# The first modulation as split products for half of its weights, with x transposed to SBUF ahead of it

## The chip, the cores and the metric

The kernel runs on one core of a Trainium2 chip. The metric is device time in microseconds (us) of that core, from the start of the program to its end. The time before is the median of three runs, 1361.34 us (1361.11 to 1365.02).

The engines are named as in the profile: PE (TensorE, matrix products and transposes), PEld (its weight loads), DVE (VectorE), ACT (ScalarE), POOL (GpSimd), and SP, whose queue issues most DMAs. An engine works through its own queue in order. SBUF is the on-chip memory, PSUM the accumulator memory that TensorE writes.

## The reference

The kernel computes a trunk of two layers on 512 tokens of width 1024, in fp32. Layer 0 mixes tokens by differential attention (four heads; 256 context tokens are keys and values too) on one half of the width and by a Fourier transform on the other, layer 1 by a long convolution; each layer ends in a gated feed-forward part with a convolution. The change touches the very beginning:

```python
def ada_params(cvec, w, b):
    m = jax.nn.silu(cvec) @ w + b
    return jnp.split(m[..., None, :], N_MOD, axis=-1)      # N_MOD = 6 pieces of 1024

def modulate(x, shift, scale):
    return layer_norm(x) * (1 + scale) + shift
...
sh1, sc1, g1, sh2, sc2, g2 = ada_params(c, mod_w[0], mod_b[0])
h_lat = modulate(x, sh1, sc1)                               # 512 x 1024
csh1, csc1, ... = ada_params(c_ctx, mod_w[0], mod_b[0])
h_ctx = modulate(ctx, csh1, csc1)                           # 256 x 1024
p = h_lat @ w_in                                            # query, key, value, Fourier part
kv_c = h_ctx @ w_in[:, DA_W:3 * DA_W]                       # key and value of the context
```

Piece 0 of the modulation is the shift, piece 1 the scale, piece 2 the gate `g1`; pieces 0 and 1 are wanted for two vectors, `c` and `c_ctx`. The filter of the convolution in layer 1 begins with three small products, each followed by a sine (`hdn = jnp.sin(fr * (... @ w + b))`); these too are computed in the first 45 us of the kernel.

## The kernel before

*Split products.* Large products are not computed on fp32 operands. An operand x is taken apart into a high part, x rounded to the type fp32r, and a low part, x minus the high part, also as fp32r. `split` (L212) does so: ScalarE copies with a cast (L213), VectorE subtracts (L210, in `sub`). `mm3` (L239) then forms three products, low x high, high x low and high x high, into one PSUM bank. `wsplit` (L231) does it for a raw weight tile of 128x2048 in two halves of 128x1024. Raw weight tiles come from `raw` (L195), which has three buffers and loads on SP's queue.

*Order.* The code is written as Python generators that are stepped in turn, but the order in which an engine's instructions stand is set by a scheduler, which takes the program in the order written as priority. `behind` (L216) tells it that what is issued inside shall stand behind the instructions listed in `self.fence`. A tile pool gives each tag a number of buffers; a new tile in a full tag waits for the readers of the oldest.

*Start* (`start`, L410). SP's queue loads the eight raw chunks of pieces 1 and 0 (two k rows of 128x1024 each, `load_mods`) and x as two tiles of 128x2x1024 (`load_x`), interleaved. `cT` holds silu of both vectors as two columns for each of eight k. `mods(piece)` (L454) forms, for each chunk, four fp32 products 2x512 (`pm`, L461: `cT[:, k]` against a half row), 32 over both pieces; copies the two-row result to `m2`, transposes it back to columns in `pmt` (L471), and adds the bias. `norm` normalizes x row-wise in place by `plain_norm` (L523: two statistics, square root on ScalarE, reciprocal, and one VectorE `tensor_scalar`, L531). `filter_head` (from L583) runs the filter's three products (`pz`, L595), each followed by `sine`: eight VectorE operations on `sa` (L574 to L579) and the sine itself on ScalarE (L580). `lift(k)` transposes the k-th column block of x into PSUM (`pt`, L491; three banks), `fill(k)` applies scale and shift out of PSUM, on ScalarE for even k (L501) and on VectorE for odd, and splits the result into `th` and `tl`. Three `lift` come ahead of the last chunks of piece 0, the other five one by one between the `fill`s.

*Attention's first stage* (`attention`, L693). `project_qk(0)` forms head 0's query (`pq`) by `mm3` over eight k, with rotary embedding in `roped` (L775 to L779, on VectorE). Then the context rows `xc` are loaded and normalized, and `gate_rows` (L533) forms the gate as sixteen fp32 products of one row, copies it to SBUF, and spreads it over the partitions (`pmr`, L545 and L546). The key follows (`pk`), then `context` (L555): in two halves, eight transposes of `xc` into a PSUM bank and four conversions, each a ScalarE activation to `fc` (two buffers), a cast to `ch` and a VectorE low part to `cl`. The context's key product (`pkc`) reads `ch` and `cl` k by k. Then come the values (`project_tokens`), and the attention proper, the rest of the layer and layer 1, none of which the change rewrites. In the background VectorE sums further modulation pieces into `acc` (`mod_jobs`, L278 and L280).

## Time and profile before

| | |
|---|---|
| time, median of three runs | 1361.34 us (1361.11 to 1365.02) |
| profiled execution, its own time | 1366.71 us |
| its span | 1364.9 us |
| TensorE busy | 1318.6 us, 97% |
| VectorE busy | 971.3 us, 71% |
| ScalarE busy | 585.9 us, 43% |
| GpSimd busy | 32.9 us, 2% |
| mean granted TensorE clock | 0.984 |

The trace is of one execution, which was 5.4 us longer than the median, so differences between stages are taken within it. A busy TensorE isn't one at its peak: the granted clock, in shares of 2.4 GHz, stands in a column of its own, and at 0.5 the same product takes twice as long. An fp32 product stands in the trace as two records, a product of fp32r as one. An idle time in brackets is that of the same engine just before the instruction, with what ended it.

### The profile page before, as it was taken

The page shows a single profiled execution, that of the slowest core. Times are in us where ns is not written, and L with a number is a line of the kernel's source. Part 1 is how long each engine was busy: PE and PEld are TensorE (multiplying, and loading weights), DVE is VectorE, ACT ScalarE, POOL GpSimd, SP SyncE. Part 2 cuts the span into 40 slices and gives each one's busy share as a digit, 9 for nine tenths or more (in the row PEclk, how much of TensorE's full clock was granted, in tenths as well). Part 3 has the DMA queues.
Part 4 walks back from the last instruction along what each step waited for, and adds up shares of the span by engine and source line. Part 5 has one row for each costly group of instructions (what it writes and reads, how often), then busy time and mean ns, then how long its engine had stood idle before and what let it go on. Part 6 is the DMA issues. An engine that isn't in the chain of part 4 may idle for free. (4 is left out here: it accounts for less than half of the span.)

```text
span 1364.9 us, 16745 instructions
## 1 busy us (share of the span) xinstructions
PE 1318.6 (97%) x6719; PEld 1092.7 (80%) x6719; DVE 971.3 (71%) x1418; ACT 585.9 (43%) x878; POOL 32.9 (2%) x44
## 2 busy tenths in 40 slices
PE   7999999989999999999999999999999999999997
PEld 1478889878887888888888878888888888888886
DVE  4667788676879975896666688899777555577545
ACT  2544545555545533433345533334563333333332
POOL 0000000000011000000000100000000000000000
PEclk9899999989999999999999999999999999999999
DMA  9562024053744554663243653232555222233201
GB/s 354 183 232 99 32 104 151 1 203 126 258 167 153 204 199 172 218 217 111 99 157 108 249 175 116 93 109 88 197 195 185 93 93 93 96 104 109 93 31 62
DMA packets 42253, 195.52 MB, mean 143 GB/s; under 512 B 4204, under 2 KB 5822, under 8 KB 29375
## 3 DMA queue, kind: packets, MB, share of 16 engines
q1 hardware_dynamic: 39522, 184.57, 38.6%
q0 software_dynamic: 1824, 8.66, 1.9%
q10 hardware_dynamic: 829, 1.21, 0.3%
q8 instruction: 53, 0.87, 0.2%
q14 instruction: 25, 0.20, 0.0%
HBM read 181.85 MB, written 12.58 MB: 142 GB/s over the span
## 5 line engine op out<-in xcount | busy, mean ns | idle before, releaser
L1086 ACT ACTIVATE u<-pf,pp 128x512 f32<-128x512 f32 x90 | 70.2, 781 | 123.5 <-PE pf L244 70.2
L1087 DVE SCALAR_TENSOR_TENSOR u<-pf,pp,u 128x511 f32<-128x511 f32 x90 | 67.0, 745 | 30.2 <-ACT u L1086 30.0
L278 DVE SCALAR_TENSOR_TENSOR acc<-mw,cT,acc 128x1024 f32<-128x1024 f32 x66 | 84.6, 1282 | 5.0 <-DMA mw<-in_modw 4.7
L966 DVE TENSOR_TENSOR wo<-wo,g 128x1024 f32<-128x1024 f32 x60 | 72.0, 1217 | 5.8 <-DMA wo<-in_dao 3.7
L210 DVE TENSOR_TENSOR sl<-hid,sh 128x512 fp32r<-128x512 f32 x39 | 26.8, 690 | 62.2 <-ACT sh L213 62.2
L213 ACT CAST sh<-hid 128x512 fp32r<-128x512 f32 x39 | 24.0, 621 | 103.8 <-PE py L997 100.7
L1088 DVE SCALAR_TENSOR_TENSOR u<-pf,pp,u 128x511 f32<-128x511 f32 x90 | 67.2, 746 | 1.9
L1038 DVE SCALAR_TENSOR_TENSOR y<-x,py 128x1024 f32<-128x1024 f32 x16 | 19.5, 1219 | 26.3 <-PE py L997 26.3
L863 ACT ACTIVATE e<-blk,nm 128x768 f32<-128x768 f32 x32 | 28.6, 900 | 22.2 <-DVE nm L860 18.0
L1040 ACT ACTIVATE junk<-y,sv 128x1024 f32<-128x1024 f32 x16 | 18.4, 1152 | 41.3 <-DVE sv L1039 41.3
L461 PE MATMUL pm<-mw,cT 128*2 128x512 f32 x64 | 31.1, 637 | 3.9 <-DVE cT L448 3.9
L860 DVE TENSOR_REDUCE nm<-blk 128x1 f32<-128x768 f32 x32 | 29.2, 946 | 4.5 <-PE blk L855 4.3
L1114 DVE TENSOR_TENSOR hid<-u 128x512 f32<-128x512 f32 x44 | 30.7, 697 | 2.1 <-ACT u L1111 0.2
L1070 DVE TENSOR_SCALAR f<-pt,mod,mod 128x128 f32<-128x128 f32 x48 | 16.4, 403 | 20.3 <-ACT f L1072 20.3
L1111 ACT ACTIVATE u<-u 128x512 f32<-128x512 f32 x44 | 27.4, 623 | 0.0
L461 PEld LDWEIGHTS pm<-mw,cT 128*2 128x2 f32 x64 | 5.2, 88 | 25.4 <-issue 21.4
L854 PE MATMUL blk<-ks,ql 128*128 128x512 f32 (+1 forms) x64 | 21.5, 353 | 1.2 <-DVE ks L210 0.7
L1072 ACT ACTIVATE f<-pt,mod,mod 128x128 f32<-128x128 f32 x48 | 18.0, 455 | 9.2 <-PE pt L1058 9.2
L1052 ACT ACTIVATE y<-x,sv 128x1024 f32<-128x1024 f32 x12 | 13.9, 1155 | 18.2 <-DVE sv L1051 18.1
L855 PE MATMUL blk<-ks,qh 128*128 128x512 f32 (+1 forms) x64 | 21.1, 348 | 0.0
L1042 DVE SCALAR_TENSOR_TENSOR x<-y,sv,ln 128x1024 f32<-128x1024 f32 x16 | 20.6, 1285 | 0.7
L1043 DVE SCALAR_TENSOR_TENSOR x<-x,sv,ln 128x1024 f32<-128x1024 f32 x16 | 20.5, 1284 | 0.6
(1102 smaller groups left out, 4402.3 us busy)
## 6 DMA issues: line engine op xcount, KB each, us to landing
mw<-in_modw SPq DMA_DIRECT2D x48, 1024.0 KB, 5.0
wi<-in_ffi SPq DMA_DIRECT2D x44, 1024.0 KB, 5.0
wo<-in_ffo SPq DMA_DIRECT2D x22, 1024.0 KB, 5.0
wv<-in_hyxv SPq DMA_DIRECT2D x8, 1024.0 KB, 5.0
xd<-x SPq DMA_DIRECT2D x12, 512.0 KB, 2.8
x<-xd SPq DMA_DIRECT2D x12, 512.0 KB, 4.6
wqk<-in_daqk SPq DMA_DIRECT2D x4, 1024.0 KB, 5.9
wo<-in_dao SPq DMA_DIRECT2D x4, 1024.0 KB, 5.0
```

What stands on the lines that cost most here:

```text
L210: return e.tensor_tensor(lo, src, hi.bitcast(F32), op=ALU.subtract)
L213: return self.nc.scalar.copy(hi, src), self.sub(lo, src, hi, eng)
L278: nc.vector.scalar_tensor_tensor(acc, ws, c, acc, op0=ALU.mult, op1=ALU.add)
L461: nc.tensor.matmul(ps[0:2, h], self.cT[:, k], w, start=(k == 0), stop=(k == KD - 1))
L860: nc.vector.tensor_reduce(nm[s], ps[s], axis=AX.X, op=ALU.max, negate=True)
L863: nc.scalar.activation(e[s], ps[s], AF.Exp, bias=nm[s], accum_out=su[s])
L966: nc.vector.tensor_tensor(w[:, ws], w[:, ws], gate, op=ALU.mult)
L1086: nc.scalar.activation(out, ps, AF.Identity, scale=w[:, 1:2], bias=w[:, 3:4])
L1087: nc.vector.scalar_tensor_tensor(out[:, 1:], ps[:, : L - 1], w[:, 0:1], out[:, 1:], op0=ALU.mult, op1=ALU.add)
L1088: return nc.vector.scalar_tensor_tensor(out[:, : L - 1], ps[:, 1:], w[:, 2:3], out[:, : L - 1], op0=ALU.mult, op1=ALU.add)
L1111: nc.scalar.activation(u[:, 0], u[:, 0], AF.Gelu)
L1114: nc.vector.tensor_tensor(hid[j // 2][:, j % 2], u[:, 0], u[:, 1], op=ALU.mult)
```

## The change

It has six parts.

1. Chunks 0 and 2 of each of the pieces 1 and 0 (`PARTED`) are taken apart by `wsplit`, and each of their fp32 products becomes two fp32r products: the high part of the weights against four columns (`c4`: high and low part of both vectors), and the low part against two. The sum has four rows for 512 columns, so `m2` and `pmt` are wider, and the two parts are added with the bias.
2. The norm of x ends with a ScalarE activation in place of the VectorE operation (`plain_norm` with `act`).
3. All eight column blocks of x are transposed and copied to SBUF (`f1`) before the modulation's last chunks; `fill` works from there. For k = 2 and 5 the low part is formed on GpSimd.
4. The three steps of the filter's head are spread among the chunks, each behind the last product of the chunk ahead of it. The second half of the query weights is split behind `fill(1)`.
5. The context rows are loaded by one DMA at the end of the start, into the buffer that `cl` takes over later (`Late`), and normalized behind the last `fill`, by ScalarE too. `context` issues all sixteen transposes first, then the eight conversions.
6. `gp`, a column wanted by the attention's last step, is formed behind a fence, and not ahead of the start's first products; the PSUM pool of the start waits tile by tile (`reuse_waits`), and one more raw chunk of piece 0 goes to a buffer of `raw`.

```diff
--- before.py
+++ after.py
+    PARTED = {1: (0, 2), 0: (0, 2)}
...
-            cl = hp.pool.tile([128, KD, LC], F32R, name="cl")
+            xc = hp.pool.tile([128, 2, D], F32, tag="cl", name="xc")
+            cl = Late(lambda: hp.pool.tile([128, KD, LC], F32R, tag="cl", name="cl"))
...
-            if n < 3:
+            if n < 3 or n == 7:
...
-            for i in range(2):
-                mw[piece, k + i] = w[:, i]
+            mw[piece, k] = w
...
+        up = {0: self.bank("sc", 3, "pt")}
+        c4 = self.cst.tile([128, KD, 4], F32R, name="c4")
+        self.split(c4[:, :, 0:2], c4[:, :, 2:4], self.cT)
...
-                self.plain_norm(xn[i][:, t], f"{i}{t}")
+                self.plain_norm(xn[i][:, t], f"{i}{t}", True)
...
             ps = self.bank("pm", 2, f"pm{piece}", 2)
-            m2 = self.cst.tile([128, 2, 512], F32, tag=("gate", "acc")[piece], name=f"m2{piece}")[0:2]
+            m2 = [self.cst.tile([128, D], F32, tag=t, name=f"m2{piece}{t}")[0:4, 0:512] for t in ("gate", "acc")]
+            mm = nc.tensor.matmul
             for c in range(0, KD, 2):
+                parted = c // 2 in self.PARTED[piece]
+                if parted:
+                    hs, ls = self.wsplit(mw[piece, c].rearrange("p a d -> p (a d)"), f"mw{piece}{c}")
-                    for k in (c, c + 1):
-                        w = mw[piece, k][:, h * 512 : (h + 1) * 512]
-                        nc.tensor.matmul(ps[0:2, h], self.cT[:, k], w, start=(k == 0), stop=(k == KD - 1))
+                    half = slice(h * 512, (h + 1) * 512)
+                    for i in range(2):
+                        k = c + i
+                        f, e = k == 0, k == KD - 1
+                        if parted:
+                            mm(ps[0:4, h], c4[:, k], hs[i][:, half], start=f, stop=False, skip_group_check=True)
+                            j = mm(ps[0:2, h], c4[:, k, 0:2], ls[i][:, half], start=False, stop=e, skip_group_check=True)
+                        else:
+                            w = mw[piece, c][:, i, half]
+                            j = mm(ps[0:2, h], self.cT[:, k], w, start=f, stop=e, skip_group_check=True)
+                self.fence = (j,)
                 yield
-            nc.scalar.copy(m2[:, 0], ps[0:2, 0])
-            nc.vector.tensor_copy(m2[:, 1], ps[0:2, 1])
+            nc.scalar.copy(m2[0], ps[0:4, 0])
+            nc.vector.tensor_copy(m2[1], ps[0:4, 1])
             pt = self.bank("po", 1, f"pmt{piece}")
             o = MODB0 + piece * 8
...
-                        pt[:, 2 * x : 2 * x + 2], m2[:, h, m * 128 : (m + 1) * 128], self.ident[0:2, 0:2]
+                        pt[:, 4 * x : 4 * x + 4], m2[h][:, m * 128 : (m + 1) * 128], self.ident[0:4, 0:4]
                     )
             for i in range(2):
-                nc.vector.tensor_tensor(ms[i], pt[:, i:16:2], self.pp[:, o : o + 8], op=ALU.add)
-                if piece == 1:
-                    nc.vector.tensor_scalar(ms[i], ms[i], 1.0, None, op0=ALU.add)
+                nc.vector.tensor_tensor(ms[i], pt[:, i:32:4], self.pp[:, o : o + 8], op=ALU.add)
+                nc.vector.scalar_tensor_tensor(
+                    ms[i], ms[i], 1.0 if piece == 1 else 0.0, pt[:, i + 2 : 32 : 4], op0=ALU.add, op1=ALU.add
+                )
...
-        up = {}
-
         def lift(k):
-            up[k] = self.bank("sc", 3, "pt")
...
+            up[k] = p.tile([128, L], F32, tag=f"f1{k}", name=f"f1{k}")
+            nc.scalar.copy(up[k], ps)
-            f = p.tile([128, L], F32, tag="f1", bufs=2, name=f"f1{k}")
+            f = up[k]
             if k % 2:
-                nc.vector.tensor_scalar(f, up[k], sc, sh, op0=ALU.mult, op1=ALU.add)
+                nc.vector.tensor_scalar(f, f, sc, sh, op0=ALU.mult, op1=ALU.add)
             else:
-                nc.scalar.activation(f, up[k], AF.Identity, scale=sc, bias=sh)
-            self.split(th[:, k, :], tl[:, k, :], f)
-
-        ms, mb = mods(1), mods(0)
+                nc.scalar.activation(f, f, AF.Identity, scale=sc, bias=sh)
+            self.fence = self.split(th[:, k, :], tl[:, k, :], f, "pool" if k in (2, 5) else "dve")
+
+        ms, mb, hd = mods(1), mods(0), self.filter_head(p)
+        step(hd, 1)
         step(ms, 1)
-        for _ in self.filter_head(p):
-            pass
+        step(hd, 1)
         step(ms, 1)
+        step(hd, 1)
         norm(1)
-        step(ms, 3)
+        step(ms, 1)
+        step(hd, 1)
+        step(ms, 1)
+        step(ms, 1)
+        step(hd, 1)
+        step(mb, 1)
+        step(mb, 1)
         norm(2)
-        step(mb, 2)
-        for k in range(3):
+        step(mb, 1)
+        for k in range(KD):
             lift(k)
-        step(mb, 3)
-        self.first = self.wsplit(self.raw(I["daqk"][0], "wqk0"), "wqk0")
+        step(mb, 1)
+        step(mb, 1)
+        raw = self.raw(self.I["daqk"][0], "wqk0")
+        self.first = [], []
+
+        def weights(i):
+            h, l = (self.wtile(f"w{x}", [128, 1024], f"wqk0{x}{i}") for x in "hl")
+            self.split(h, l, raw[:, i * 1024 : (i + 1) * 1024])
+            for a, t in zip(self.first, (h, l)):
+                a.append(t)
+
+        weights(0)
+        nc.sync.dma_start(xc, I["ctx"].rearrange("(t p) d -> p t d", p=128))
         for k in range(KD):
             fill(k)
-            if k + 3 < KD:
-                lift(k + 3)
+            if k == 1:
+                with self.behind():
+                    weights(1)
+        with self.behind():
+            for t in range(2):
+                self.plain_norm(xc[:, t], f"0{t}", True)
         return th, tl
-    def plain_norm(self, x, name):
+    def plain_norm(self, x, name, act=False):
...
-        nc.vector.tensor_scalar(x, x, mu, r, op0=ALU.subtract, op1=ALU.mult)
+        if act:
+            nc.vector.scalar_tensor_tensor(mu, mu, -1.0, r, op0=ALU.mult, op1=ALU.mult)
+            nc.scalar.activation(x, x, AF.Identity, scale=r, bias=mu)
+        else:
+            nc.vector.tensor_scalar(x, x, mu, r, op0=ALU.subtract, op1=ALU.mult)
...
+        pts = []
         for half in range(2):
-            pt = self.bank("blk", 2, "blk", 3).rearrange("p a b -> p (a b)")
+            pts.append(self.bank("blk", 2, "blk", 3).rearrange("p a b -> p (a b)"))
...
-                    self.nc.tensor.transpose(pt[:, o : o + 128], xc[t][:, c : c + 128], self.ident)
-            for k in range(4):
-                kk = 4 * half + k
-                sc, sh = (self.mods[0, x, 1][:, kk : kk + 1] for x in (1, 0))
-                f = self.p.tile([128, LC], F32, tag="e0", bufs=2, name="fc")
-                self.nc.scalar.activation(f, pt[:, k * LC : (k + 1) * LC], AF.Identity, scale=sc, bias=sh)
-                self.split(ch[:, kk, :], cl[:, kk, :], f)
+                    self.nc.tensor.transpose(pts[half][:, o : o + 128], xc[:, t, c : c + 128], self.ident)
+        cl.make()
+        for kk in range(KD):
+            k = kk % 4
+            sc, sh = (self.mods[0, x, 1][:, kk : kk + 1] for x in (1, 0))
+            f = self.p.tile([128, LC], F32, tag="e0", bufs=2, name="fc")
+            self.nc.scalar.activation(f, pts[kk // 4][:, k * LC : (k + 1) * LC], AF.Identity, scale=sc, bias=sh)
+            self.split(ch[:, kk, :], cl[:, kk, :], f)
...
-            nc.tensor.matmul(ps, fw[0:66, 0] if i == 0 else fw[:, i], cur, start=True, stop=True)
+            with self.behind():
+                nc.tensor.matmul(ps, fw[0:66, 0] if i == 0 else fw[:, i], cur, start=True, stop=True)
...
+            yield
...
-        gp = self.sm.tile([128, 1], F32, name="gp")
-        nc.vector.tensor_scalar(gp, self.pp[:, SG0 : SG0 + 1], POST, None, op0=ALU.mult)
...
-        xc = []
...
-                for t in range(2):
-                    xc.append(p.tile([128, D], F32, tag=f"pt{t}", name=f"xc{t}"))
-                    nc.sync.dma_start(xc[t], I["ctx"][t * 128 : (t + 1) * 128])
-                    self.plain_norm(xc[t], f"0{t}")
...
+        self.gp = self.sm.tile([128, 1], F32, name="gp")
+        with self.behind():
+            nc.vector.tensor_scalar(self.gp, self.pp[:, SG0 : SG0 + 1], POST, None, op0=ALU.mult)
...
+class Late:
+    def __init__(self, make):
+        self.tile = None
+        self.new = make
+
+    def make(self):
+        self.tile = self.new()
+
+    def __getitem__(self, at):
+        return self.tile[at]
```

The first place is on TensorE, in the modulation: how the split products stand among the fp32 ones. `pm` is the sum of one piece, `mw..h` and `mw..l` are high and low part of a chunk's half, `pz` is the filter head's product, `pt` a transposed block of x. Before:

```order
L461 MATMUL pm_134<-mw_102,cT 2x512 x4
L461 MATMUL pm_247<-mw_106,cT 2x512 x4
L461 MATMUL pm_247<-mw_108,cT 2x512 x2
L595 MATMUL pz<-hd_160,fw 128x256
L461 MATMUL pm_247<-mw_108,cT 2x512
L471 MATMUL pmt_218<-ident,m_135 128x2 x8
L461 MATMUL pm_247<-mw_108,cT 2x512
```

After:

```order
L472 MATMUL pm_264<-mw00h_271,c_131 4x512
L473 MATMUL pm_264<-mw00l_268,c_131 2x512
L472 MATMUL pm_264<-mw00h_271,c_131 4x512
L473 MATMUL pm_264<-mw00l_272,c_131 2x512 x2
L476 MATMUL pm_264<-mw_108,cT 2x512 x2
L641 MATMUL pz<-hd_181,fw 128x256
L476 MATMUL pm_264<-mw_108,cT 2x512
L487 MATMUL pmt_241<-ident,m21gate 128x4 x4
L487 MATMUL pmt_241<-ident,m21acc 128x4 x4
L476 MATMUL pm_264<-mw_108,cT 2x512
L506 MATMUL pt<-ident,xin_104 128x128 x3
L472 MATMUL pm_264<-mw04h_303,c_131 4x512 x2
```

In place of fp32 products of whole chunks, the last five fp32r products of chunk 0 of piece 0 stand in a row, and behind them two fp32 products ahead of the third `pz`. The transposes of the first piece's sums (`pmt`) and the first ones of x follow in between.

The second place is on VectorE, at the same time: the third sine of the filter's head (`sa`, lines 616 to 624 in the code after) and what stands around it. `mw00l` is a low part of the weights, `mod` the modulation's columns. Before, the second sine with the statistics and the norm of x:

```order
L527 BN_STATS st_240<-xin_104 128x6
L578 SCALAR_TENSOR_TENSOR sa_161<-sa_161 128x256
L464 COPY m_135<-pm_134 2x512
L578 SCALAR_TENSOR_TENSOR sa_161<-sa_161 128x256
L263 RECIPROCAL st_233<-st_233 128x1
L529 BN_AGGR st_240<-st_240 128x2
L578 SCALAR_TENSOR_TENSOR sa_161<-sa_161 128x256
L531 TENSOR_SCALAR xin_104<-xin_104,st_233 128x1024
L579 TENSOR_SCALAR sa_161<-sa_161 128x256
L263 RECIPROCAL st_240<-st_240 128x1
L531 TENSOR_SCALAR xin_104<-xin_104,st_240 128x1024
```

After, the second and the third:

```order
L623 SCALAR_TENSOR_TENSOR sa_182<-sa_182 128x256
L211 TENSOR_TENSOR mw00l_268<-mw_106,mw00h_267 128x1024
L623 SCALAR_TENSOR_TENSOR sa_182<-sa_182 128x256
L211 TENSOR_TENSOR mw00l_272<-mw_106,mw00h_271 128x1024
L624 TENSOR_SCALAR sa_182<-sa_182 128x256
L571 SCALAR_TENSOR_TENSOR st_287<-st_287 128x1
L568 BN_AGGR st_295<-st_295 128x2
L619 TENSOR_SCALAR sa_226<-pz,fb 128x256
L620 TENSOR_SCALAR sa_226<-sa_226 128x256
L621 TENSOR_SCALAR sa_226<-sa_226 128x256
L491 TENSOR_TENSOR mod_242<-pmt_241,pp 128x8
```

The two low parts of 128x1024 stand between the last operations of the second sine, the norm's long `TENSOR_SCALAR` on x is gone from the queue, and the third sine, which waits for `pz`, stands ahead of the operations that read `pmt`.

The third place is on VectorE around head 0's key: `pk` is the key's product in PSUM, lines 776 to 779 (819 to 822 after) its rotary embedding, `cl` the low parts of the context, `acc` a sum of mod_jobs. Before:

```order
L210 TENSOR_TENSOR cl<-fc,ch 128x256 x4
L280 TENSOR_SCALAR acc_908<-mw_909,cT 128x1024
L278 SCALAR_TENSOR_TENSOR acc_908<-mw_909,cT,acc_908 128x1024
L776 STREAM_SHUFFLE k_497<-pk 128x512
L777 TENSOR_TENSOR kf_471<-pk,rope 128x512
L778 TENSOR_TENSOR k_497<-k_497,rope 128x512
L779 TENSOR_TENSOR kf_471<-kf_471,k_497 128x512
L210 TENSOR_TENSOR cl<-fc,ch 128x256 x2
L210 TENSOR_TENSOR wqk1l_782<-wqk_779,wqk1h_781 128x1024
L278 SCALAR_TENSOR_TENSOR acc_908<-mw_1005,cT,acc_908 128x1024
L210 TENSOR_TENSOR cl<-fc,ch 128x256 x2
L278 SCALAR_TENSOR_TENSOR acc_908<-mw_1005,cT,acc_908 128x1024
```

After:

```order
L819 STREAM_SHUFFLE k_561<-pk 128x512
L820 TENSOR_TENSOR kf_535<-pk,rope 128x512
L821 TENSOR_TENSOR k_561<-k_561,rope 128x512
L211 TENSOR_TENSOR cl<-fc,ch 128x256
L822 TENSOR_TENSOR kf_535<-kf_535,k_561 128x512
L211 TENSOR_TENSOR cl<-fc,ch 128x256
L279 SCALAR_TENSOR_TENSOR acc_975<-mw_1072,cT,acc_975 128x1024
L211 TENSOR_TENSOR cl<-fc,ch 128x256 x2
L279 SCALAR_TENSOR_TENSOR acc_975<-mw_1072,cT,acc_975 128x1024
L211 TENSOR_TENSOR cl<-fc,ch 128x256 x2
L211 TENSOR_TENSOR wqk1l_849<-wqk_846,wqk1h_848 128x1024
L211 TENSOR_TENSOR cl<-fc,ch 128x256 x2
```

Before, four `cl` stand ahead of the rotary embedding, which waits for `pk`; after, none does, and the first comes between its operations.

## Rows read from the trace of the kernel before

**Rows 1.** The page: span, engines' busy time, one group of its part 5.
```profile
span 1364.9 us, 16745 instructions
PE 1318.6 (97%) x6719; PEld 1092.7 (80%) x6719; DVE 971.3 (71%) x1418; ACT 585.9 (43%) x878; POOL 32.9 (2%) x44
...
L1052 ACT ACTIVATE y<-x,sv 128x1024 f32<-128x1024 f32 x12 | 13.9, 1155 | 18.2 <-DVE sv L1051 18.1
```

**Rows 2.** Stages: start:end, length, busy PE, PEld, DVE, ACT, POOL, clock, DMA share, GB/s.
```profile
8.90:43.50 34.60, 34.56 (x90) 7.94 (x90) 19.92 (x51) 10.63 (x17) 0.00 (x0) 1.00 0.89 342
43.50:51.00 7.50, 4.47 (x29) 3.34 (x28) 5.97 (x11) 5.33 (x8) 0.00 (x0) 0.83 0.29 120
51.00:58.60 7.60, 7.60 (x26) 5.89 (x25) 4.11 (x6) 3.92 (x5) 1.04 (x2) 0.72 0.66 224
58.60:72.50 13.90, 13.90 (x33) 2.60 (x32) 8.37 (x21) 6.15 (x10) 0.00 (x0) 1.00 0.61 203
75.90:83.10 7.20, 7.20 (x27) 5.79 (x28) 3.14 (x5) 2.12 (x6) 0.00 (x0) 0.77 0.72 255
83.10:90.30 7.20, 6.42 (x53) 6.03 (x51) 7.01 (x12) 4.13 (x10) 0.00 (x0) 1.00 0.25 104
300.00:1364.90 1064.90, 1045.47 (x5196) 882.46 (x5194) 762.96 (x1075) 439.42 (x636) 26.13 (x30) 0.99 0.41 142
```

**Rows 3.** Timeline, 8 to 46 us: start, duration, engine, line, operation, [idle before].
```profile
8.59 0.15 DVE L707 TENSOR_SCALAR gp<-pp 128x1 f32<-128x1 f32 x1 [7.66 <-DMA pp<-in_pp]
8.94 6.25 PE L461 MATMUL pm<-mw,cT 128*2 128x512 f32 x8 [3.94 <-DVE cT L448]
12.89 1.88 DVE L527 BATCH_NORM_STATS2 st<-xin 128x6 f32<-128x512 f32 x3 [4.01 <-DMA xin<-in_x]
15.74 7.03 PE L461 MATMUL pm<-mw,cT 128*2 128x512 f32 x16
35.12 1.53 PE L491 MATMUL pt<-ident,xin 128*128 128x128 f32 x12
45.02 0.78 ACT L501 ACTIVATE f<-pt,mod,mod 128x512 f32<-128x512 f32 x1 [2.52 <-DVE mod L475]
```

**Rows 4.** Groups by line, 0 to 60 us: busy us, mean ns | idle before.
```profile
L213 ACT CAST m0h<-f 128x512 fp32r<-128x512 f32 x8 | 4.9, 619 | 0.5 <-DVE f L499 0.2
L213 ACT CAST wqk0h<-wqk 128x1024 fp32r<-128x1024 f32 x2 | 2.0, 1042 | 0.0
L210 DVE TENSOR_TENSOR wqk0l<-wqk,wqk0h 128x1024 fp32r<-128x1024 f32 x2 | 2.4, 1221 | 0.9 <-ACT wqk0h L213 0.9
L210 DVE TENSOR_TENSOR m0l<-f,m0h 128x512 fp32r<-128x512 f32 x8 | 5.4, 689 | 0.8 <-ACT m0h L213 0.7
L531 DVE TENSOR_SCALAR xin<-xin,st 128x1024 f32<-128x1024 f32 x4 | 3.2, 805 | 0.0
L580 ACT ACT_TABLE_LOAD x2 | 2.6, 1283 | 0.0
```

**Rows 5.** The three sines' instructions alone (tile `sa`), 0 to 43.5 us.
```profile
0.00:43.50 43.50, 7.84 (x21) 1.25 (x3) 1.00 0.87 330
```

**Rows 6.** Timeline, 70 to 92 us.
```profile
72.84 1.00 ACT L546 COPY acc<-blk 1x1024 f32<-1x1024 f32 x1
83.20 0.73 DVE L776 STREAM_SHUFFLE k<-pk 128x512 f32<-128x512 f32 x1
85.74 0.76 DVE L210 TENSOR_TENSOR cl<-fc,ch 128x256 fp32r<-128x256 f32 x2
86.55 1.23 DVE L210 TENSOR_TENSOR wqk1l<-wqk,wqk1h 128x1024 fp32r<-128x1024 f32 x1
87.70 1.28 DVE L278 SCALAR_TENSOR_TENSOR acc<-mw,cT,acc 128x1024 f32<-128x1024 f32 x1
89.36 0.39 PE L243 MATMUL pkc<-cl,wqk0h 128*128 128x256 f32 x1 [0.78 <-DVE cl L210]
```

**Rows 7.** Line 657: ns min/median/max of one, first and last start.
```profile
L657 POOL TENSOR_TENSOR nacc<-nacc,h x12: 736/743/1655, 381.0 to 476.8; 128x256 f32<-128x256 f32 x12
```

More of the change, by code (lines that the diff above doesn't have):

```diff
@@ L348, in run @@
             ch = hp.pool.tile([128, KD, LC], F32R, name="ch")
-            cl = hp.pool.tile([128, KD, LC], F32R, name="cl")
+            xc = hp.pool.tile([128, 2, D], F32, tag="cl", name="xc")
+            cl = Late(lambda: hp.pool.tile([128, KD, LC], F32R, tag="cl", name="cl"))
             mp = enter_pool(self.pool("mT"))
             mT = Cols(mp.pool, [4, 5, 6, 7, 0, 1, 2, 3], "mT")
-            with tc.tile_pool(name="ps0", bufs=1, space=PSUM) as self.ps:
+            with self.pool("ps0", space=PSUM) as self.ps:
                 with self.pool("start") as sp:
-                    th, tl = self.start(sp)
+                    th, tl = self.start(sp, xc)
             with self.pool("ps1", space=PSUM) as self.ps:
@@ L357, in run @@
                 with self.pool("att") as self.p:
-                    fp, rest = self.attention(th, tl, ch, cl, mT, hp)
+                    fp, rest = self.attention(th, tl, ch, cl, xc, mT, hp)
                 fp.close()
@@ L705, in attention @@
         nc.vector.tensor_scalar(nlam, nlam, -LAM0, None, op0=ALU.add)
-        gp = self.sm.tile([128, 1], F32, name="gp")
-        nc.vector.tensor_scalar(gp, self.pp[:, SG0 : SG0 + 1], POST, None, op0=ALU.mult)
-        self.rope, self.nlam, self.gp = rope, nlam, gp
+        self.rope, self.nlam = rope, nlam
         self.first_blk = self.bank("blk", 2, "blk", 3)
-        xc = []
         self.qk, self.v = {}, {}
```

7 lines of the change are left out of this document (4 added, 3 removed).

## The prediction

> **What bounds the kernel now.** I read the page first: TensorE is busy for 1318.6 of 1364.9 us [rows 1]. Then busy time by stage [rows 2]: from 300 us on, TensorE works 1045.5 of 1064.9 us, so whatever this change gains or loses in the first 90 us, where all its instructions stand, is handed on nearly one to one. Before 90 us the stages have different limits. From 8.9 to 43.5 TensorE is full (34.56 of 34.60): the fp32 modulation products. From 43.5 to 51.0 it works 4.47 of 7.5 us, because `fill` waits for the modulation; behind that gap the granted clock is down (mean 0.72 from 51.0 to 58.6). 58.6 to 72.5 is the gate row, full. From 75.9 to 83.1 head 0's key product runs at a mean clock of 0.77, and from 83.1 to 90.3 TensorE works 6.42 of 7.2 us while VectorE works 7.01: VectorE sets that stage. The timeline shows its last wait: 0.78 us at 89.36 for `cl` [rows 6].
>
> **Prices.** An fp32 product of 512 columns stands in the trace as two records: 16 records in 7.03 us make 0.88 us each at 2.4 GHz, 8 in 6.25 us make 1.56 in the slow first microseconds [rows 3]. An fp32r product of 512 columns: 24 of them fill 7.2 us at a mean clock of 0.77 [rows 2], so 7.2 x 0.77 / 24 = 0.23, and 0.46 at 1.2 GHz. A split of 128x1024 costs ScalarE 1.04 and VectorE 1.22; one of 128x512 0.62 and 0.69 [rows 4]. One sine of the filter head takes VectorE 7.84 / 3 = 2.6 and ScalarE 1.25 / 3 = 0.42 [rows 5], plus a table load of 1.28 [rows 4].
>
> **The modulation, by sums.** 16 of 32 fp32 products become 32 fp32r ones. Four of them run slow: 4 x 1.56 - 8 x 0.46 = 2.6; twelve fast: 12 x 0.88 - 24 x 0.23 = 5.0. TensorE loses 7.6 us of work. Eight splits add 8.3 us to ScalarE and 9.8 to VectorE. Four norms leave VectorE (4 x 0.81 = 3.2 [rows 4]) for ScalarE; the trace has no such activation from SBUF to SBUF with a column as scale, and the nearest rows bound it by 1.04 (the cast of that size) and 1.155 (the square, [rows 1]); I take 1.1, so 4.4. Square root and sine now alternate three times and not twice: two table loads more, 2.6. ScalarE comes to 10.6 + 8.3 + 4.4 + 2.6 = 26, VectorE to 19.9 + 9.8 - 3.2 = 26.5, TensorE to 27, all under the 34.6 us of the stage. By sums the modulation would be early. The order decides otherwise, because three sines, each a trip TensorE, VectorE, ScalarE and back, are now threaded with four trips ScalarE, VectorE, TensorE of the splits, on queues that run in order.
>
> **The modulation, by its chain.** The first x tile lands at 12.89 [rows 3]. VectorE then has four statistics (0.63 each), the first sine, the two low parts of the third chunk and some small operations of 0.15: 2.5 + 2.6 + 2.4 + 0.9, to 21.3. TensorE follows with two split products, one fp32 product and the sine's product of half its size: 0.46 + 0.88 + 0.44, to 23.1. VectorE: second sine, three statistics, the copy of the first sums, two low parts, 2.6 + 1.9 + 0.7 + 2.4 + 0.5, to 31.2. ScalarE 0.42. TensorE has two split products from 31.0, two fp32 ones ahead of the third sine's product: 0.46 + 1.76 + 0.44, to 33.7. VectorE's third sine is interleaved with the four operations that read `pmt1`, which stands behind one more fp32 product and eight small transposes, to 35.2; what is left of the sine, then the last two low parts, 2.2 + 2.7, to 40.1. TensorE: 0.46, four fp32 products 3.5, and 23 transposes at 0.13 (12 in 1.53 [rows 3]) 3.0, to 47.1; `pmt0` and the sums, 1.0: 48.1. ScalarE's nine copies of 0.6 behind the first of these transposes end at 48.3 too. The first `fill` starts at 45.02 now [rows 3]. The modulation is late by 3.2 us, not early.
>
> **Fill and query product.** Before, ScalarE and VectorE take turns with TensorE's transposes; now all eight tiles lie in SBUF. ScalarE's queue is the limit: four activations, eight casts, and one cast of weights, 12 x 0.62 + 1.04 = 8.5, to 56.8; the last low part at 57.5, the last products at 59.2. Before it was 58.6. But five of the gate row's sixteen products have run in the gaps.
>
> **Gate row to key product.** 11 x 0.88 = 9.7, to 68.9 (before 72.5). Its sum is then copied by ScalarE, in whose queue the copy stands behind two casts of value weights and the query halves, and these behind the rope of the query on VectorE, which now comes after four statistics of the context: 57.5 + 2.5 + 2.5 (four rope operations: 83.20 to 85.74 in the key's rope [rows 6]) + 2.0 of small ones = 64.5; exponential 0.3 behind its table load and the context's two norms, done by 66.5; 2 x 0.62 + 2 x 1.04 + 0.62 + copy 1.00 [rows 6], to 71.4. So the context's norms, done before in the shade of the gate row, now put a wait of 1.6 us after it. Two products of 0.88: the key product begins at 73.3, against 75.9. I give it the same mean clock as before, since the same transposes and a longer wait stand ahead of it: 7.2 us, to 80.5, 2.6 early.
>
> **Context conversion.** The gain ends here. `context` converts through a buffer of two, so the third `fc` needs the first `cl` done. Before, four `cl` were done ahead of the key's rope; now none is: the scheduler put the first `cl` between the rope's operations, and these wait for the key product's end. VectorE behind the product now has rope 2.5, eight `cl` at 0.38 (pairs of 0.76), two accumulations of 1.28 and a low part of 1.23 [rows 6], 9.3; ScalarE's turns add 0.5, TensorE's rest 0.6: 80.5 + 10.4 = 90.9. Before it was 83.1 + 7.1 = 90.2. Four `cl`, one accumulation and the waits eat the lead: +0.7.
>
> **Clock.** In the chain above TensorE ends the second chunk's three other fp32 products (2.6) at 25.8, and has then only six split products and three transposes, some 1.8 us, until 31.0. The trace shows what follows such a stretch: 4.47 us busy in 7.5, then a clock of 0.72 on average [rows 2]. A fall as long as the one in the key product (7.2 x 0.23 x 2 = 3.3 us at 1.2 GHz) lengthens the chain by at most 1.7. I take 1.3, as some of it meets a wait. The Trainium skill (TensorE: Matmul & The Clock Gate, HAM oscillation — how this bites in real kernels) says the same in general: gaps between groups of matmuls bring the throttle back and every group then starts cold. That rule speaks against a change that trades full TensorE work for gaps; by it alone, with each of the two gaps paid in full, the sum below would be 2 us higher.
>
> **Low parts on GpSimd.** Tiles 2 and 5 get theirs there. The nearest row, half that size, took 0.736 to 1.655 us [rows 7], so 1.5 to 3.3 each. At 1.5 both are there when TensorE comes to them (54.5 and 56.0); at 3.3 the second comes at 59.6 and the query is 2.6 later. I take 1.5, twice the median of 0.743. The Trainium skill (GPSIMD Engine Reference, 1. Specifications) says that GpSimd shares its SBUF interfaces with VectorE, with contention when a VectorE instruction has two SBUF inputs, as the low parts beside it do. The spread in that row would fit; by the rule the sum is the 2.2 of the next rival higher.
>
> **Rest.** The load of x, the modulation weights and the query weights are bound by transfers that land before use; the context's load, a megabyte, is issued once the query weights are, far ahead of its use. `gp` no longer holds the first product (VectorE waited for its load until 8.59 [rows 3]); the split of the first chunk takes that up, and the first product begins at 10.1, not 8.94 [rows 3]; the chain hides it. Later orders differ in a few places only; I take 0, with 1.3 either way, the price of one accumulation put ahead of another operation.
>
> **Sum.** +0.7 + 1.3 = +2.0. The profiled execution took 1366.71 us around a span of 1364.9, so 1368.7 in its own terms; it stands 5.4 above the median of the runs, 1361.34, and against that the forecast is **1363.3**, with 1360 to 1366 if its mechanism is right.
>
> **Rivals.** *TensorE stays the bound* (chance 0.15): if the three engines' trips overlap better than my chain says, the modulation takes TensorE's work alone, 34.6 - 7.6 + 2.6 for twenty transposes that come ahead, from 10.1 to 39.7, and 40.7 with the sums, 7.4 before my 48.1. Then 2.0 - 7.4 = -5.4: 1356.0. For it: no engine's sum reaches the stage. Against it: the second and third sine wait for products behind the split ones.
> *TensorE at half clock through the modulation* (0.20): the work from 31.0 to 48.1 in the chain is 3.5 + 1.5 and 0.5 + 3.5 + 3.0 + 0.7, 12.7 us; with half of it at 1.2 GHz the chain grows by 6.3 in place of 1.3: 2.0 + 5.0 = +7.0, 1368.3. It decides from a granted clock under 0.75 over 28 to 48 us. For it: TensorE is under half busy from 26 to 31 and again from 37 to 40.5. Against it: between them are fp32 products back to back, and such a run had full clock throughout 8.9 to 43.5.
> *GpSimd contention* (0.15): the query 2.6 late, of which 0.4 falls into the wait for the second tile: +2.2, so +4.2: 1365.5.
> *The change does as it says but the context's wait isn't there* (0.10): if VectorE gets through `cl` as quickly as before, 2.6 - 1.3 of the lead is kept: -1.3, 1360.0.
>
> **Chances.** My forecast has 0.40. A difference under 0.3% (4.1 us) can't be told from none: 1357.3 to 1365.4. Faster takes the first rival and a little of the last, 0.16; slower the clock rival, half of GpSimd's and a tail of mine, 0.28; the rest is 0.56. The range 1357.0 to 1369.0 leaves out two thirds of the first rival, and the upper end of the clock's.
>
> **What would show it.** Right: first `fill` at 47 to 50 us, gate copy later than the gate row's last product by over 1 us, the first `cl` after the key's shuffle, TensorE waiting for `cl` three times or more around 82 to 90, the key product's last product 2 to 4 us early and the value products of the context within 3 us of before. Wrong: modulation done before 45, a key product that ends 6 us early, or a stage after 100 us whose length changes by more than 2 us.

## The result and the profile after

The changed kernel took 1374.83 us (median of four runs, 1370.91 to 1376.85) beside 1362.94 us of the kernel before: a ratio of 1.0082 with a 95% interval of 1.0064 to 1.0100. A later set of five runs gave 1373.67 us, ratio 1.0086 (1.0063 to 1.0109). The forecast was 1363.3 with a range up to 1369.0: the change is slower, by some 12 us in the medians (11 by the ratio) and not by 2.

The page of the changed kernel; its profiled execution took 1376.85 us. TensorE is busy 4.5 us longer than in [rows 1], and the span is 10.2 us longer.

```profile
span 1375.1 us, 16789 instructions
PE 1323.1 (96%) x6719; PEld 1091.4 (79%) x6719; DVE 975.3 (71%) x1427; ACT 604.3 (44%) x902; POOL 35.5 (3%) x46
```

The same stages as in [rows 2], with the same columns, at this kernel's own limits: modulation, gap, query, gate row, gate's spreading, key, the context's key, and from 300 us on.

```profile
9.70:44.30 34.60, 30.53 (x91) 7.67 (x91) 22.81 (x56) 23.55 (x31) 0.00 (x0) 0.95 0.83 329
44.30:49.70 5.40, 4.89 (x33) 2.89 (x32) 2.96 (x9) 4.47 (x10) 0.00 (x0) 1.00 0.61 196
49.70:59.65 9.95, 9.72 (x31) 4.48 (x32) 8.26 (x13) 7.72 (x12) 3.73 (x4) 1.00 0.66 224
59.65:69.15 9.50, 9.50 (x23) 1.73 (x22) 4.59 (x17) 6.50 (x9) 0.00 (x0) 1.00 0.71 241
69.15:74.60 5.45, 4.02 (x13) 1.66 (x12) 2.93 (x3) 4.62 (x8) 0.00 (x0) 0.81 0.95 347
74.60:82.40 7.80, 7.80 (x26) 6.21 (x26) 2.04 (x2) 1.21 (x2) 0.00 (x0) 0.70 0.54 206
82.40:92.50 10.10, 7.61 (x52) 6.39 (x51) 8.88 (x16) 5.96 (x13) 0.00 (x0) 1.00 0.25 77
300.00:1375.10 1075.10, 1055.79 (x5203) 885.43 (x5201) 762.18 (x1074) 440.15 (x637) 25.70 (x30) 0.99 0.41 140
```

The modulation is as long as before though TensorE works four us less in it, the gate row is over 3.3 us sooner, and the context's key needs 10.1 us and not 7.2. From 300 us on TensorE is busy 10.3 us longer than in [rows 2]; 1.6 us of that is work that it has still to do because it is late at 300 us, the rest falls on the same products. The timeline has the places that the forecast named.

```profile
9.72 0.59 PE L472 MATMUL pm<-mw10h,c 128*4 128x512 f32 x1 [4.82 <-DVE c L211]
...
28.50 0.58 PE L473 MATMUL pm<-mw00l,c 128*2 128x512 f32 x1 [1.11 <-DVE mw00l L211]
...
47.80 0.82 ACT L518 ACTIVATE f<-f,mod,mod 128x512 f32<-128x512 f32 x1 [0.32 <-DVE mod L491]
...
52.44 2.69 POOL L211 TENSOR_TENSOR m0l<-f,m0h 128x512 fp32r<-128x512 f32 x2 [51.13 <-ACT m0h L214]
...
70.62 1.00 ACT L589 COPY acc<-blk 1x1024 f32<-1x1024 f32 x1
...
71.67 3.00 PE L594 MATMUL pmr<-acc,ones 2*128 2x512 f32 x4 [1.43 <-ACT acc L589]
...
84.41 0.42 DVE L211 TENSOR_TENSOR cl<-fc,ch 128x256 fp32r<-128x256 f32 x1
...
84.88 0.39 PE L244 MATMUL pkc<-cl,wqk0h 128*128 128x256 f32 x1 [1.34 <-DVE cl L211]
...
87.35 0.39 PE L244 MATMUL pkc<-cl,wqk0h 128*128 128x256 f32 x1 [0.55 <-DVE cl L211]
...
91.22 0.39 PE L243 MATMUL pkc<-ch,wqk0l 128*128 128x256 f32 x1 [0.44 <-ACT ch L214]
```

The first value product of x, before and after:

```profile
93.66 0.28 PE L242 MATMUL pv<-wv0h,m0l 128*128 128x256 f32 x1
```

```profile
95.94 0.28 PE L243 MATMUL pv<-wv0h,m0l 128*128 128x256 f32 x1
```

The start has lost 2.3 us. But matched product by product, the difference grows where no instruction has changed. Up to 350 us it moves with stretches in which the granted clock is 1.2 and not 2.4 GHz ("falls of the clock"), which do not stand at the same places in the two traces: it is 0.2 us at 200, 1.65 at 350 and 3.3 at 375 (one more fall in the trace after, at 352). Then it is 4.7 at 600, 6.9 at 1025, 10.07 at the end. Between 375 and 1350 us that is 6.8 us, with the same falls in both traces. It comes in patches that return with every fifth weight chunk (a chunk is a weight tile of the feed-forward parts with its 48 products). The 13th and 37th product of two chunks next to each other, before and after:

```profile
535.83 0.39 PE L242 MATMUL pf<-f0h,wi014l 128*128 128x512 f32 x1
...
541.27 0.39 PE L242 MATMUL pf<-f0h,wi014l 128*128 128x512 f32 x1
...
548.55 0.39 PE L242 MATMUL pf<-f0h,wi015l 128*128 128x512 f32 x1
...
553.99 0.39 PE L242 MATMUL pf<-f0h,wi015l 128*128 128x512 f32 x1
```

```profile
540.06 0.39 PE L243 MATMUL pf<-f0h,wi014l 128*128 128x512 f32 x1
...
545.50 0.39 PE L243 MATMUL pf<-f0h,wi014l 128*128 128x512 f32 x1
...
552.80 0.40 PE L243 MATMUL pf<-f0h,wi015l 128*128 128x512 f32 x1
...
558.40 0.40 PE L243 MATMUL pf<-f0h,wi015l 128*128 128x512 f32 x1
```

24 products take 5.44 us, 0.2267 each, in chunk 14 and 5.60 us, 0.2333 each, in chunk 15. Before, both took 5.44. Of the chunks from 10 to 20, after, 10, 15 and 20 take 5.60, 12, 13, 17 and 18 between 5.49 and 5.53, and the other four 5.44; before, all take 5.44.

### The profile page after: what moved, and what is told of

Same layout as the page of the kernel before. It is cut to its first block, busy times and chain, and to the rows that moved or that the text cites. A ratio compares the mean times of both kernels' runs of the same rounds, so it can differ in the third digit from the quotient of the medians.

```text
span 1375.1 us, 16789 instructions
## 1 busy us (share of the span) xinstructions
PE 1323.1 (96%) x6719; PEld 1091.4 (79%) x6719; DVE 975.3 (71%) x1427; ACT 604.3 (44%) x902; POOL 35.5 (3%) x46
## 5 line engine op out<-in xcount | busy, mean ns | idle before, releaser
L1081 DVE SCALAR_TENSOR_TENSOR y<-x,py 128x1024 f32<-128x1024 f32 x16 | 19.5, 1219 | 29.1 <-PE py L1040 29.1
L1095 ACT ACTIVATE y<-x,sv 128x1024 f32<-128x1024 f32 x12 | 13.8, 1154 | 18.2 <-DVE sv L1094 18.1
L264 DVE RECIPROCAL sv<-sv 128x1 f32<-128x1 f32 x32 | 5.1, 160 | 21.5 <-ACT sv L263 21.5
L214 ACT CAST yh<-ya 128x512 fp32r<-128x512 f32 x16 | 9.9, 618 | 22.4 <-DVE ya L1247 22.4
```

What stands on the lines that cost most here:

```text
L214: return self.nc.scalar.copy(hi, src), self.sub(lo, src, hi, eng)
```

## The experiments

Two theories stood against each other. A: the new tile `c4` has 128 bytes per partition, which shifts all tiles of the left-hand pools by 128 bytes, but not those of the right-hand pools; the ring of weight tiles has five buffers, one of them on the right. By the layout of the compiled program the first high half of chunk 15 lies on the right (at byte 221152) and its low half on the left (68448); those of chunk 14 all lie on the left. A chunk has four weight tiles (high and low part of two halves): of these, chunks 10, 15 and 20 have two on the right, chunks 12, 13, 17 and 18 one, the other four none, which is the pattern of the patches. Before, all places left the same rest by 256; there chunk 14 has two tiles on the right, and it took 5.44 us, so the right side by itself costs nothing. B: the new order of the start leaves something behind.

How the table is read: each run lists its span and the mean granted clock. (1 - clock) x span is the time that the falls of the clock cost at most; the trace shows them as pieces that cost up to 1.7 us each, in numbers that differ from run to run. The rest of a run's time ("outside") repeats better: in the kernel before its mean is 1345.1 to 1345.4 on four chips. The last column is counted against that of the same chip (one of 28 runs there, with a clock of 0.964, is left out); for the changed kernel, against the mean of the four. The columns falls and outside are means; a clock of three digits leaves 0.7 us of doubt in one run, and the standard error of an entry of the last column is 0.2 to 0.7 us.

The division is not exact. Among the runs of the kernel before, the time grows by 0.7 to 0.9 us for each us of falls (0.67, 0.72, 0.87 and 0.71 on the four chips) and not by 1, so a part of the falls costs nothing; I take it that these meet waits. A version with more falls than another looks somewhat too good in the last column, and differences of 1 to 2 us in it are to be read with that in mind.

| kernel | runs | median us | ratio (95%) | falls | outside, over before |
|---|---|---|---|---|---|
| before | 101 | 1361.9 to 1363.1 | | 18.1 | 0 |
| changed, both sets | 9 | 1374.8, 1373.7 | 1.008 | 18.9 | +10.4 |
| 1, 13: shift of 256 | 6, 12 | 1372.4, 1369.0 | 1.0069 (1.0053 to 1.0086), 1.0047 (1.0032 to 1.0061) | 23.1, 19.7 | +3.9, +4.7 |
| 2: before, shift of 128 | 6 | 1369.7 | 1.0053 (1.0035 to 1.0071) | 18.7 | +6.1 |
| 3: before, shift of 64 | 8 | 1367.1 | 1.0038 (1.0020 to 1.0057) | 19.5 | +3.6 |
| 4: no split, shift of 256 | 12 | 1364.0 | 1.0010 (0.9997 to 1.0022) | 17.0 | +1.7 |
| 5: xc in its own buffer | 8 | 1367.2 | 1.0036 (1.0022 to 1.0049) | 19.8 | +1.9 |
| 6: context as before | 6 | 1370.7 | 1.0065 (1.0048 to 1.0082) | 22.6 | +3.0 |
| 7: no split, context as before | 7 | 1367.7 | 1.0039 (1.0022 to 1.0056) | 17.4 | +5.2 |
| 8: no split, own buffer | 12 | 1362.8 | 1.0000 (0.9988 to 1.0013) | 17.9 | -0.3 |
| 10, 16: as 8, gate copy first | 12, 12 | 1359.9, 1360.5 | 0.9983 (0.9967 to 1.0000), 0.9980 (0.9966 to 0.9994) | 16.3, 17.2 | -0.8, -1.2 |
| 11: as 5, gate copy first | 11 | 1364.8 | 1.0016 (1.0003 to 1.0030) | 18.7 | +1.0 |
| 12, 14: as 1, with filler | 11, 12 | 1368.8, 1368.7 | 1.0032 (1.0013 to 1.0052), 1.0037 (1.0023 to 1.0051) | 18.3, 17.0 | +4.9, +6.3 |
| 15: as 11, with filler | 12 | 1363.4 | 0.9998 (0.9985 to 1.0012) | 16.1 | +2.3 |

**Place of the tiles (1, 2, 3, 9).** One line makes a tile wider, by 128 bytes in the changed kernel and in the one before (48 columns), and by 64 in the one before (32 columns):

```diff
-        self.cT = self.cst.tile([128, KD, 2], F32, name="cT")
+        self.cT = self.cst.tile([128, 48], F32, name="cT")[:, 0:16].rearrange("p (k s) -> p k s", s=2)
```

> The changed kernel with 128 bytes per partition more in the pool of constants (cT made wider and not used), so that the tiles of the left-hand pools stand 256 bytes further than in the kernel before, and not 128. Theory A (relative place of tiles): the new tile c4 has 128 bytes per partition, which shifted all tiles of the left-hand pools by 128 bytes against those of the right-hand pools; every fifth pair of weight halves of the feed-forward parts mixes both, and its products take 0.2335 us in place of 0.2268. With 256 bytes all stand as before to each other: spacing 0.2268 in all chunks, no growth of the difference after 375 us, ratio 1.001 to 1.003 (the 1.6 to 2.3 us that the start has lost). Theory B (the new order of the start leaves something behind, a clock or a queue, or it is the chip of that run): unchanged, ratio 1.007 to 1.009, and the difference goes on growing by 0.3 us in each 25 us.

> The kernel before with 128 bytes per partition more in the pool of constants (cT wider, not used), nothing else. Theory A: the same loss without any of the change: slow halves where one weight tile lies in the right-hand pool, 0.2335 against 0.2268 us, ratio 1.005 to 1.007. Theory B: ratio 0.999 to 1.001.

> The kernel before with 64 bytes per partition more. Theory A: a loss too, between 0 and that of 128 bytes if the distance counts in steps, the same if any unequal place counts; ratio 1.002 to 1.007. Theory B: 0.999 to 1.001.

The timeline of the first, chunk 15, whose slow patch is gone:

```profile
554.96 0.39 PE L243 MATMUL pf<-f0h,wi015l 128*128 128x512 f32 x1
...
560.40 0.39 PE L243 MATMUL pf<-f0h,wi015l 128*128 128x512 f32 x1
```

The timeline of the second, where chunk 14 now has the tiles on both sides:

```profile
532.61 0.40 PE L242 MATMUL pf<-f0h,wi014l 128*128 128x512 f32 x1
...
538.21 0.40 PE L242 MATMUL pf<-f0h,wi014l 128*128 128x512 f32 x1
...
545.57 0.39 PE L242 MATMUL pf<-f0h,wi015l 128*128 128x512 f32 x1
...
551.01 0.39 PE L242 MATMUL pf<-f0h,wi015l 128*128 128x512 f32 x1
```

The timeline of the third, the same chunk 14:

```profile
532.92 0.40 PE L242 MATMUL pf<-f0h,wi014l 128*128 128x512 f32 x1
...
538.44 0.40 PE L242 MATMUL pf<-f0h,wi014l 128*128 128x512 f32 x1
```

Theory A holds: a shift alone slows the kernel before, in the chunks whose tiles lie on both sides (5.60 us for 24 products), and 256 bytes heal the changed one (5.44). With 64 bytes the same chunk takes 5.52 us, half the loss. Outside the falls the price is 10.4 less 4.4 (experiments 1 and 13), 6.0 us. The traces say it without that division: matched product by product from 375 to 1350 us, with the same falls in both, experiment 2 loses 6.9 us against the kernel before and experiment 9 loses 6.8 against 13, while 13 loses nothing there against the kernel before. The expected ratio of the first (1.001 to 1.003) was missed all the same, and its 1.0069 lies at the edge of what theory B expected: more was lost in the start than I thought, and in falls. Experiment 9 is the changed kernel again:

> The changed kernel unchanged, beside the next ones on one chip, for its time outside falls of the clock (1356.2 us in four runs, 7.0 over the first experiment) and for what its falls cost. Theory (relative place of tiles): time outside the falls 1355 to 1357, falls 18 to 23 us, ratio 1.007 to 1.010. Rival (the first four were one chip's): within 2 us of the first experiment's 1349.2.

It gave 1355.1 us outside, 19.5 of falls and a ratio of 1.0086, as the theory said.

**Split products (4).** With the shift of 256 kept and the sums of two rows again:

```diff
-    PARTED = {1: (0, 2), 0: (0, 2)}
+    PARTED = {1: (), 0: ()}
```

> The changed kernel with 256 bytes of shift in all and with no chunk of the modulation as split products (PARTED empty, two-row sums as before); x transposed ahead, norms on ScalarE and the context's early load stay. Theory of the prediction (the chain through sines and splits makes the modulation late): modulation done by 45 to 46 us and the first fill no later than 46.5; the difference at the value products under +1; ratio 0.999 to 1.001. Rival (the context's wait makes the loss, whatever the modulation does): first fill at 45 but the value products still 1.5 to 2.5 us late, ratio 1.001 to 1.003.

The first fill starts at 46.19 us, the value products at 92.58, 1.1 us sooner than before, and the ratio is 1.0010: by these signs the prediction's theory holds. But this trace has one piece of falls up to there and that of before three, so that without them the value products would be some 2.3 us late, as the rival says; TensorE waits 1.42 us for the gate copy, then 1.34, 0.56 and 0.43 us for the context. So both cost something. On one chip each, the split products make the median 4.4 us longer (5 against 8) and 4.9 us (11 against 10). By the table 2.2 and 1.8 us of that stand outside the falls (and 2.2 from 4 to 1), 1.9 and 2.4 us in them (and 6.0 from 4 to 1, but the falls of 1 were fewer when it was run again as 13). How it divides is not shown: in the traces the value products start 0.3 us sooner in 5 than in 8, and 1.9 later in 11 than in 10 with one more piece of falls.

**The context's buffer (5, 8).** With the shift of 256, and one buffer in place of two for the sine's scratch tile to make room:

```diff
-            xc = hp.pool.tile([128, 2, D], F32, tag="cl", name="xc")
+            xc = hp.pool.tile([128, 2, D], F32, name="xc")
```

> The changed kernel with 256 bytes of shift, and the context rows xc in a buffer of their own in place of the one that cl takes over (the sine's scratch tile has one buffer, not two, to make room). Theory A (the buffer makes the context wait: no cl can be written before all sixteen transposes of xc are done, and eight of them stand behind the key product): four cl go ahead of the key's rope again, the waits for cl in the context's key product fall from about 2.3 us to under 1, the value products of x start 1.5 to 2.5 us sooner than in the first experiment; the time outside falls of the clock goes from 3.8 us over that of before to about 1.5 to 2. Theory B (the two buffers of fc make the wait): no change.

> As the fourth experiment (no split products, 256 bytes of shift), with xc in a buffer of its own. Theory A: the wait for cl goes, 1.5 to 2.5 us sooner than the fourth, ratio to before 0.998 to 1.000. Theory B: as the fourth, 1.001.

VectorE in experiment 5, around the key's rope:

```profile
71.73 0.42 DVE L211 TENSOR_TENSOR cl<-fc,ch 128x256 fp32r<-128x256 f32 x1 [0.88 <-ACT ch L214]
72.52 0.42 DVE L211 TENSOR_TENSOR cl<-fc,ch 128x256 fp32r<-128x256 f32 x1 [0.37 <-ACT ch L214]
...
74.92 0.76 DVE L211 TENSOR_TENSOR cl<-fc,ch 128x256 fp32r<-128x256 f32 x2 [0.40 <-ACT ch L214]
...
81.31 0.73 DVE L819 STREAM_SHUFFLE k<-pk 128x512 f32<-128x512 f32 x1
```

Four `cl` stand ahead of the shuffle again, with two buffers of `fc` as ever, and the ratio of 8 is 1.0000: theory A holds in both. What held them was the buffer of `cl` itself: it is free only when all sixteen transposes of `xc` are done, and eight of these stand behind the key product. In the traces TensorE waits 0.80 us for the context in 5 and in 8, and 2.3 in 1 and in 4. Price outside the falls: 2.0 us (1 less 5, and 4 less 8; each pair is on two chips).

**Part 5 undone (6, 7).** Load, norm and conversion of the context rows as in the kernel before.

> The changed kernel with 256 bytes of shift and part 5 undone: context rows loaded, normalized and converted as in the kernel before; the split products, the transposes ahead and the rest stay. If part 5 makes the start's loss: value products of x at or ahead of those of before, time outside falls of the clock 0 to 1 us over before. If the modulation's chain makes it: unchanged, 3 to 4 us over before.

> 256 bytes of shift, no split products and the context as before; what is left of the change are the norms on ScalarE, the transposes of x ahead of the modulation, the low parts on GpSimd, the filter's head spread out and gp later. If these parts are worth something by themselves: ratio 0.996 to 0.999. If the lead of the gate row is lost again in the context's conversion, whose first cl stands behind the key's shuffle here too: ratio 0.999 to 1.002, as in the fourth experiment.

Neither gains what was hoped. The gate row is early now, and TensorE waits for the norm in its place: 1.80 and 0.53 us ahead of the transposes of `xc` in experiment 6, 2.21 and 0.53 in experiment 7. Without split products undoing part 5 costs 3.5 us outside the falls (7 less 4), so the early load is worth something there; with them 6 can't be told from 1 and 13, and what the load is worth stays open.

**Gate copy first (10, 11, 16).** On top of 8 and 5:

```diff
-        nc.scalar.copy(acc[0:1].rearrange("p (a b) -> p a b", a=2), ps[0:1, 0:2])
+        self.fence = (nc.scalar.copy(acc[0:1].rearrange("p (a b) -> p a b", a=2), ps[0:1, 0:2]),)
...
+        with self.behind(name == "v0"):
+            hs, ls = self.wsplit(self.raw(self.I["davf"][which, pair], "w" + name), "w" + name)
...
+            with self.behind(h == 0):
```

> As the eighth experiment (no split products, xc in its own buffer, 256 bytes of shift), and the casts of the value weights and the query halves put behind the copy of the gate's sum on ScalarE. If that copy's place in the queue makes TensorE wait 1.4 to 1.8 us after the gate's products: wait under 0.5 us, gate spread over the partitions and key product 1.3 to 1.8 us sooner, and with the shorter wait one fall of the clock less at 70 to 80 us (3.4 us); ratio 0.996 to 0.998. If the wait only moves on to the conversions of the context: ratio 0.999 to 1.001.

> The same with the split products of the change kept (the fifth experiment with the copy ahead). Time outside falls of the clock 1345.5 to 1346.5 where the wait is what held it, ratio 1.001 to 1.003; unchanged at 1347.2 where the wait moves on.

> The tenth experiment again, to settle whether it beats the kernel before: 1 to 3 us faster, ratio 0.998 to 0.999, interval under 1.

In experiment 8 TensorE waits for the copy of the gate's sum:

```profile
70.71 2.90 PE L593 MATMUL pmr<-acc,ones 2*128 2x512 f32 x4 [1.80 <-ACT acc L588]
```

In experiment 10 ScalarE waits for the gate's products and not TensorE for the copy:

```profile
68.55 1.00 ACT L588 COPY acc<-blk 1x1024 f32<-1x1024 f32 x1 [2.16 <-PE blk L584]
```

Its stages from 66 to 76 us, in the columns of [rows 2]:

```profile
66.00:70.00 4.00, 3.93 (x15) 1.48 (x14) 0.31 (x2) 1.83 (x4) 0.00 (x0) 1.00 0.96 285
70.00:76.00 6.00, 6.00 (x18) 4.01 (x17) 4.20 (x7) 5.98 (x14) 0.00 (x0) 0.72 0.42 167
```

The wait of 1.80 us is gone, and in these two traces one piece of falls of two in this stage. Without split products this version is faster than the kernel before by 2.0 and 2.4 us in the medians, 0.2%; the interval of the first (0.9967 to 1.0000) just reaches 1, that of the repetition (0.9966 to 0.9994) does not. The 0.996 to 0.998 expected of experiment 10 was just missed; 11 and 16 came out as expected. With split products (11) it is 2.9 us slower than the kernel before.

**Filler in the wait (12, 13, 14, 15).** Four products whose result nobody reads:

```diff
+        with self.behind():
+            ps = self.bank("sc", 3, "junk")
+            for i in range(4):
+                nc.tensor.matmul(ps[0:2], self.cT[:, i], mw[1, 6][:, i % 2, 0:512], start=True, stop=True)
         step(mb, 1)
```

> The first experiment (change with 256 bytes of shift) with four fp32 products more, of no use, between the last chunk of piece 1 and the first of piece 0, where TensorE waits for the split. If that wait brings the fall of the clock at 28 to 34 us: full clock there, modulation done no later than before, cost of falls 1.7 us lower. If the falls come from elsewhere: no change in them, and the time is that of the first experiment or up to 1.5 us more.

> The first experiment again (change with 256 bytes of shift), now beside the one with the filler on one chip. Theory (the wait ahead of chunk 0 of piece 0 brings falls of the clock): falls cost 22 to 24 us, time outside them 1348.5 to 1349.5. Rival (the 23.1 us of the first experiment were that chip's): 17 to 19 us.

> The twelfth experiment again: four useless fp32 products in that wait. Theory: falls cost 3 to 5 us less than beside it without them, and the whole is 3 us faster in spite of the added work. Rival: same falls, and 0 to 1 us slower.

> The eleventh experiment (split products, xc in its own buffer, gate copy first, 256 bytes of shift) with the four useless products. Theory: falls 16 to 17.5 us in place of 18.7, time 1363 to 1364 us, still not under that of the kernel before. Rival: 1365 or more.

Stages of experiment 1, behind it of 12 (with filler), and of 13, which is the kernel of 1 again:

```profile
24.00:28.00 4.00, 2.42 (x9) 0.49 (x6) 3.54 (x10) 3.95 (x6) 0.00 (x0) 1.00 1.03 410
28.00:34.00 6.00, 5.18 (x12) 0.99 (x12) 2.35 (x6) 4.78 (x6) 0.00 (x0) 0.72 1.02 412
```

```profile
24.00:28.00 4.00, 4.00 (x11) 0.77 (x9) 3.54 (x8) 3.97 (x5) 0.00 (x0) 1.00 1.03 410
28.00:34.00 6.00, 6.00 (x21) 1.51 (x20) 3.00 (x9) 4.78 (x7) 0.00 (x0) 1.00 1.02 412
```

```profile
24.00:28.00 4.00, 2.33 (x8) 0.49 (x6) 3.54 (x9) 3.95 (x6) 0.00 (x0) 1.00 1.03 410
28.00:34.00 6.00, 5.17 (x16) 1.13 (x17) 3.17 (x9) 4.79 (x6) 0.00 (x0) 1.00 1.02 411
```

The fall at 28 us is there in experiment 1 and not with the filler, but the wait does not bring it each time: experiment 13 has the same wait and full clock. Of the seven traces with split products and no filler four have it, of the three with filler none, which is too few to be sure. In the table the falls are 2.7 us less with the filler on one chip (14 against 13), 2.6 less from 11 to 15, under the 3 to 5 expected; but 1.6 and 1.3 us come back outside them, and the time is the same, 1368.7 against 1369.0 us, where 3 us less were expected. Experiment 15 came out within its 1363 to 1364. The Trainium skill (TensorE: Matmul & The Clock Gate, HAM oscillation — how this bites in real kernels) has gaps between groups of products bring the throttle back; the falls column of these runs leans that way, 2.7 us less with the gap filled, without a gain in time. The 23.1 us of the first experiment came down to 19.7 in the same kernel on another chip, between what experiment 13 expected (22 to 24) and its rival (17 to 19): why the falls differ so much between sets stays open, and with it some 3 us of any single comparison.

## Why the prediction was wrong

The step that failed is **Rest**: "Later orders differ in a few places only; I take 0, with 1.3 either way ..." The order was compared, the places of the tiles were not. That term measured +6.0 us outside the falls, and 6.8 us in the trace from 375 us on. The prediction's own sign of an error, a stage after 100 us whose length changes by more than 2 us, was met. With the places put right (experiments 1 and 13) the kernel is still 9.3 and 6.1 us slower than before and not 2.0: the sum of the start was too small as well.

The start's terms, one by one:
- *Modulation by its chain.* Forecast end 48.1, first fill 47 to 50; it was 47.30 and 47.80. Right against the rival in which TensorE stays the bound, and in part by luck: this trace has a fall at 28 us, which the forecast counts in a term of its own. In three executions without that fall (5, 9 and 13) the modulation ends at 46.4 to 46.5 and the first fill starts at 46.9 to 47.0, so the chain was some 1.6 us too long.
- *Gate row to key product.* Forecast 68.9 for the products, 71.4 for the copy, 73.3 for the key; it was 69.2, 71.6 and 74.6, since the spreading of the gate ran mostly at half clock (3.00 us, not 1.76). The key product, at a mean clock of 0.70 and not 0.77, ended 0.6 us early and not 2 to 4.
- *Context conversion.* The consequence was right (first `cl` behind the shuffle, three waits, 2.3 us), the cause wrong: `fc` has two buffers in experiment 5 as well, and the wait is gone. It was the buffer that `xc` shares with `cl`.
- *Sum of the start.* +0.7 and +1.3 were forecast, +2.3 measured at the value products, with three pieces of falls up to there in either trace. In the means it is more: 4.4 us outside the falls, some 2 of split products and 2 of the buffer among them. The four kept traces of this start have 2.3, 2.8 (9), 3.7 (1) and 3.5 us (13) there, with the falls taken off; what is left up to 4.4 stays open.
- *Clock.* +1.3 forecast, +0.8 in nine runs, less than two sets of one kernel differ by (23.1 and 19.7). The rival with half clock through the modulation was wrong: the mean clock from 28 to 48 us is 0.91, and it wanted under 0.75.
- *GpSimd.* 1.35 us for a low part against 1.5 taken; the last query product started at 59.30 (forecast 59.2), so the contention rival was wrong.
- *Norm on ScalarE.* 1.23 us, over both bounds (1.04 and 1.155) and 0.13 over the 1.1 taken: 0.5 us in four norms, which the end of the modulation does not show.

## What to carry over

A new constant can move every tile behind it. Compare the layout of the compiled program as well as the order, above all where a ring of buffers lies in two pools, and keep such pools' distance as it was by a tile's width. Where a kernel's time wanders with the clock, look at each run's falls before comparing, and take what they cost from runs of one kernel and not from their length alone. And a buffer that two tiles share is a wait on the last reader, wherever the scheduler puts that reader.
